# A decoder step on one core: queries turned at once, cached key products in two blocks, and the pooling state summed behind the first pooled tile

## The chip, the core and the metric

The kernel runs on one core of a Trainium2 chip. Matrix products run on TensorE (PE; its weight loads are PEld), other arithmetic on VectorE (DVE), ScalarE (ACT) and GpSimd (POOL); SyncE (SP) and the others issue transfers, which run on 16 DMA engines. The metric is the device time of one execution in microseconds (us); smaller is better.

## The reference

The reference computes one layer of a hybrid decoder for a prompt of 512 tokens and for 8 sample sequences that each add one token to 1,024 cached ones. Where the change sits, it is this (cut):

```
z = rmsnorm(x, g_mix) @ w_in          # pooling channels u, queries q, keys and values kv, gates
ext = concatenate([prefix, u])        # prefix: 15 earlier positions (state_pool) for the samples
win_sum = upto[P+1 : P+1+T] - cs[P+1-w : P+1-w+T]     # trailing sums, w = 2, 4, 8, 16
y_pool = einsum('btgc,gcd->btgd', win_sum / cnt - u, w_pool) * pool_scale
# samples, 8 heads on 2 key heads:
s_c = q . kvc      # compressed cached keys  -> p_c, o_c; the best blocks are chosen from p_c
s_s = q . cached keys of the chosen blocks   -> o_s
s_w = q . cache_win keys (512)               -> o_w
o = g0 * o_c + g1 * o_s + g2 * o_w
mem_kv = rmsnorm(mem_prompt, g_mem) @ w_xkv   # 256 memory tokens
```

Output projection, cross-attention and a gated MLP with a short convolution follow; they lie behind the change.

## The kernel before

Prompt and samples share each weight: a projection multiplies a weight tile of 128 x 128 with 512 prompt tokens and 8 sample tokens, in two halves of 260 columns. Numbers are kept as a high and a low part, so that each weight half is loaded (`load_in`, tile w_raw, on SyncE's queue), split into w_hi (a copy on ScalarE) and w_lo (a difference on VectorE), and then used by three products (L206): w_hi with x_hi, w_hi with x_lo, w_lo with x_hi. One tile is 8 blocks x 3 x 2 = 48 products.

The samples' cached keys come in eight pages Kt (`fetch_keys`), the window keys Wk and window values Wv by SyncE's queue, the cached values Vcmp and Vslc by GpSimd (`fetch_values`). `turn_queries` (L624) multiplies the sample queries by the compression weights, so that `cached_scores(r)` can multiply four pages of cached keys at once, on four strips of 32 rows of the array: L641 for the compressed scores (64 products), L646 for the scores of single tokens (8 products, 512 columns). `window_scores` (L662) does the same with Wk, `window_values` (L866) with Wv and the transposed weights PTw; `cmp_values` (L800, L807, L815) turns the compressed weights back into values.

The pooling group's four tiles run in the order gi = 3, 2, 1, 0. Each is projected, evicted into U, summed by doubling adds on GpSimd (4 for gi = 3, window 16), reduced by the running mean into pl_d on VectorE, and mapped by w_pool (L965) one tile later. For the samples, sums of the cached pooling state stp go to spre (L1007) and are needed by pl_d (L1013). The memory tokens' norm is taken from mrow (squares at L689) and spread to Rm; mt holds the memory tokens, and is split into mT_hi on ScalarE and mT_lo on VectorE.

The order of the work comes from generators that `merge` interleaves by their yields and weights, and a scheduler then orders each engine's instructions by what is written first and by the data they wait for. `last_on(engine)` holds an instruction behind the last one written so far for that engine, and `tc.issue_after(x)` behind x. Each queue takes its transfers in the order in which they are issued, and tiles come from pools with a few buffers.

Of the kernel before, what the change touches and what calls it, by code (L numbers as in the profile page):

```python
# [16 lines left out]
P = 128  # L17
# [3 lines left out]
NB = 8  # L21
HT = 260
# [85 lines left out]
def decoder_step(ctx: ExitStack, tc: tile.TileContext, A, O):  # L108
# [562 lines left out]
    def fetch_window_keys():  # L671
        for r in range(2):
            Wk.append(pair_tile("Wk").rearrange("p (b t) -> p b t", b=4))
            sp.dma_start(Wk[r], A["win_k_t"][:, 4 * r:4 * r + 4])

    def sample_front():
        yield from cached_scores(0)
        fetch_keys(7)
        fetch_window_keys()
        fetch_window_values(0)  # L680
        yield 3.0
        yield from window_scores()

    mrow = []

    def memory_norm():
        ssm = ptile(rp, [P, 8], "ss", bufs=2)
        for i in range(2):
            act.activation(mrow[0][:, i], mrow[0][:, i], AF.Square, accum_out=ssm[:, i:i + 1])  # L689
        vcopy(rsm, rstd_from(ssm[:, 0:2], 2))  # L690
        yield 3.0
        ps = bank("tb")
        with last_on(EN.PE):
            for i in range(2):
                pe.transpose(ps[:, i * P:(i + 1) * P], rsm[:, i:i + 1].to_broadcast([P, P]), ident)
        acopy(Rm, ps[:, 0:MEM])

    def sample_back():
        yield from cached_scores(1, 1.5)
        fetch_window_values(1)  # L700
        for ct in range(2):
            fetch_values(ct, "cmp")

# [83 lines left out]
    def cmp_values():  # L787

        PT = cmp_PT[0]
        wv = ptile(pb, [P, 8, 2, 64], "wvPT", name="wv")  # L790
        sp.dma_start(wv, A["w_cmp_t"][:, 1])
        acc = bank("s")
# [96 lines left out]
    def sample_attention():  # L889
# [12 lines left out]
        for ct in range(2):  # L902
            fetch_values(ct, "slc")
        yield from memory_norm()
        yield from cmp_values()
# [6 lines left out]
    def sample_end():  # L912
        a = sel_a[0]
        PTs = ptile(pb, [P, 16, 64], "wvPT", name="PTs")
        yield from selected_turn(a, PTs)
        new_values()
# [33 lines left out]
    def pooling():  # L950
        stp = ptile(pu, [P, 2, HT], "pl_d", bufs=4, name="stp").rearrange("p r t -> p (r t)")[:, 0:4 * NB * 15]
        stp = stp.rearrange("p (g b t) -> p g b t", g=4, b=NB)
        sp.dma_start(stp, A["state_pool_t"])
        spre = ptile(pu, [P, 4, NB], "spre")
        wpl = ptile(pu, [P, 4, P], "wpl")
        sp.dma_start(wpl, A["w_pool"][0].rearrange("g c d -> c g d"))
        ulast = ptile(pu, [P, 4, 24], "ulast")
# [10 lines left out]
        for hf in (1, 0):  # L968
            raw = raws[hf]
            for l in (1, 0):  # L970
# [17 lines left out]
                tt(u[:, 528:536].rearrange("p (r t) -> p r t", r=2), ps[:, :, 256:260], R1[:, :, 256:260], OP.mult)  # L988
                vcopy(ulast[:, gi], u[:, 512:536])
                win = 2 << gi  # L990
                cur = u[:, 0:528]
# [12 lines left out]
                if gi == 3:  # L1004
                    with last_on(EN.DVE):
                        for i in range(4):
                            dve.tensor_reduce(spre[:, i], stp[:, i, :, 16 - (2 << i):15], axis=AX.X, op=OP.add)  # L1007
# [227 lines left out]
    run(qt)  # L1235
    merge((kv_first(), 4.0), (gate_tile(w_g), 4.0), (turn_queries(), 3.0))
    raw_kv.append(load_in(12))
    fetch_keys(6)
    merge((kv_tiles(1, raw_kv[0]), 12.0), (sample_front(), 12.0))
    raw_p = load_in(2)  # L1240
    merge((kv_tiles(2, raw_kv[1]), 12.0), (sample_back(), 13.0))
    es_p0.close()
    pb, es_pb = open_pool("pb")
    pools = pooling()
    merge((sample_attention(), 24.0), ((next(pools) for _ in range(20)), 15.0))
# [532 lines left out]
```

## Time and profile before

| what | us |
|---|---|
| median of 3 runs (870.12 to 871.24) | 870.94 |
| the profiled execution's own time | 874.23 |
| its span, first to last instruction | 871.2 |
| TensorE busy | 839.8 |
| VectorE busy | 556.7 |
| ScalarE busy | 374.0 |
| GpSimd busy | 105.6 |

The profiled execution took 3.0 us more than the span that its trace shows, and 3.3 more than the median of the runs; rows of the trace are compared with the span.

### The profile page before, as it was taken

Reading aid. Unit: us, or ns where it says so; the run is one execution under the profiler, and the core shown is the slowest. Engines: PE = TensorE matmul, PEld = TensorE weight load, DVE = VectorE, ACT = ScalarE, POOL = GpSimd, SP = SyncE. Lnnn points to the kernel's source line nnn. Section 1 sums busy time; section 2 is a strip of 40 time slices with the busy share of each in tenths; the row PEclk is TensorE's granted clock in tenths of the full one; section 3 lists DMA queues with packets and bytes.
Section 4 is the critical chain, followed back from the end, with each engine's and each line's share of the span. In section 5 each row is a group of like instructions: output and inputs, shape, how many; then the busy total and the mean of one; then the engine's idle time right before and its main releaser. Section 6 shows DMA issues by size and latency. Waiting matters only on the chain.

```text
span 871.2 us, 17411 instructions
## 1 busy us (share of the span) xinstructions
PE 839.8 (96%) x7077; PEld 784.0 (90%) x7077; DVE 556.7 (64%) x1424; ACT 374.0 (43%) x692; POOL 105.6 (12%) x100
## 2 busy tenths in 40 slices
PE   8899978999999999999999999999999999999996
PEld 7897856887778799999799999999999999999995
DVE  4763427887667766888564587773367774357754
ACT  6442333566765544444243344441144342133462
POOL 4732132200000023000053000000000000000031
PEclk9989989999999999999999999999999999999997
DMA  9966964563312083577433633322233322333212
GB/s 341 285 212 229 412 247 165 149 221 112 118 64 59 4 262 129 167 241 252 136 97 128 223 105 97 97 98 77 77 90 97 98 97 98 97 94 86 63 62 98
DMA packets 108911, 126.02 MB, mean 145 GB/s; under 512 B 4680, under 2 KB 95176, under 8 KB 106640
## 3 DMA queue, kind: packets, MB, share of 16 engines
q1 hardware_dynamic: 103360, 102.37, 37.2%
q0 software_dynamic: 3600, 19.55, 6.0%
q10 hardware_dynamic: 1872, 3.00, 0.9%
q8 instruction: 55, 0.90, 0.4%
q14 instruction: 24, 0.20, 0.1%
HBM read 117.76 MB, written 10.69 MB: 147 GB/s over the span
## 4 chain that ended last, share of the span: by engine, by line
PE 83%; DMA 9%; DVE 4%; ACT 2%; issue 1%; DVEq 0%; POOLq 0%; SPq 0%; ACTq 0%
PE ps_pp L206 57%; DMA w_raw<-in_w_in_t_dram 4%; DMA w_u<-in_w_up_dram 3%; PE ps_o L1115 2%; PE ps_tb L1043 2%; PE ps_tb L1220 2%; PE ps_sc L1072 2%; PE ps_tf L1100 2%; PE ps_x L1408 1%; PE ps_x L1389 1%; PE ps_pp L1676 1%; PE ps_tb L1190 1%; DMA xrow<-in_x_row_dram 1%; PE ps_pp L1190 1%; DVE w_lo L120 1%; ACT w_hi L117 1%
## 5 line engine op out<-in xcount | busy, mean ns | idle before, releaser
L206 PE MATMUL ps_pp<-x_hi,w_hi 128*128 128x260 f32 x832 | 169.6, 284 | 0.4 <-ACT w_hi L117 0.4
L206 PE MATMUL ps_pp<-x_hi,w_lo 128*128 128x260 f32 x832 | 169.3, 284 | 0.5 <-DVE w_lo L120 0.5
L206 PE MATMUL ps_pp<-x_lo,w_hi 128*128 128x260 f32 x832 | 168.0, 283 | 0.0
L206 PEld LDWEIGHTS ps_pp<-x_hi,w_lo 128*128 128x128 f32 x832 | 128.8, 189 | 1.2 <-DVE w_lo L120 0.7
L206 PEld LDWEIGHTS ps_pp<-x_hi,w_hi 128*128 128x128 f32 x832 | 128.7, 189 | 0.9 <-ACT w_hi L117 0.6
L206 PEld LDWEIGHTS ps_pp<-x_lo,w_hi 128*128 128x128 f32 x832 | 128.1, 188 | 0.4 <-issue 0.4
L117 ACT ACTIVATE w_hi<-w_raw 128x1024 fp32r<-128x1024 f32 (+1 forms) x52 | 54.2, 1042 | 123.3 <-PE ps_pp L206 96.0
L120 DVE TENSOR_TENSOR hT<-hT,ps_pp 128x520 f32<-128x520 f32 (+1 forms) x44 | 28.4, 646 | 85.7 <-PE ps_pp L206 76.5
L117 ACT ACTIVATE w_hi<-w_u 128x1024 fp32r<-128x1024 f32 x44 | 46.7, 1061 | 77.1 <-PE ps_pp L206 65.4
L120 DVE TENSOR_TENSOR w_lo<-w_raw,w_hi 128x1024 fp32r<-128x1024 f32 (+1 forms) x52 | 64.5, 1240 | 8.4 <-ACT w_hi L117 8.0
L206 PE MATMUL ps_pp<-h_lo,w_hi 128*128 128x260 f32 x304 | 61.4, 283 | 0.0
L206 PE MATMUL ps_pp<-h_hi,w_hi 128*128 128x260 f32 x304 | 61.2, 283 | 0.0
L206 PE MATMUL ps_pp<-h_hi,w_lo 128*128 128x260 f32 x304 | 61.2, 283 | 0.0
L120 DVE TENSOR_TENSOR ext<-ps_pp,R 128x512 f32<-128x512 f32 x44 | 30.4, 691 | 45.4 <-PE ps_pp L206 45.2
L120 DVE TENSOR_TENSOR w_lo<-w_u,w_hi 128x1024 fp32r<-128x1024 f32 x44 | 53.9, 1225 | 7.3 <-ACT w_hi L117 7.1
L206 PE MATMUL ps_pp<-xn_hi,w_hi 128*128 128x260 f32 x208 | 45.6, 299 | 1.8 <-ACT w_hi L117 1.1
L206 PEld LDWEIGHTS ps_pp<-h_hi,w_hi 128*128 128x128 f32 x304 | 46.9, 188 | 0.2 <-ACT h_hi L117 0.2
L206 PEld LDWEIGHTS ps_pp<-h_hi,w_lo 128*128 128x128 f32 x304 | 46.9, 189 | 0.0
L206 PEld LDWEIGHTS ps_pp<-h_lo,w_hi 128*128 128x128 f32 x304 | 46.7, 188 | 0.0
L206 PE MATMUL ps_pp<-xn_lo,w_hi 128*128 128x260 f32 x208 | 43.8, 291 | 0.0
L206 PE MATMUL ps_pp<-xn_hi,w_lo 128*128 128x260 f32 x208 | 43.2, 288 | 0.0
L1618 POOL DMA_DIRECT2D out_ffn_t_dram<-last x1 | 0.6, 577 | 351.5 <-DVE last L114 351.5
(458 smaller groups left out, 1852.3 us busy)
## 6 DMA issues: line engine op xcount, KB each, us to landing
w_u<-in_w_up_dram SPq DMA_DIRECT2D x44, 512.0 KB, 4.3
xkr<-in_cache_mem_dram SPq DMA_DIRECT2D x16, 512.0 KB, 4.4
xvr<-in_cache_mem_dram SPq DMA_DIRECT2D x16, 512.0 KB, 7.3
w_raw<-in_w_down_dram SPq DMA_DIRECT2D x8, 1024.0 KB, 5.3
Kt<-in_k_t_dram SPq DMA_DIRECT2D x32, 128.0 KB, 2.4
w_raw<-in_w_in_t_dram SPq DMA_DIRECT2D x8, 512.0 KB, 5.2
w_raw<-in_w_xkv_dram SPq DMA_DIRECT2D x4, 1024.0 KB, 6.0
w_v<-in_w_xkv_dram SPq DMA_DIRECT2D x4, 1024.0 KB, 6.6
```

Of the source, the lines that this page charges most:

```text
L117: act.activation(o, i, AF.Copy, scale=scale)
L120: (eng or dve).tensor_tensor(o, a, b, op=op)
L206: pe.matmul(o, a[:, k, :], x[:, hf, :], start=(k == 0 and j == 0), stop=(k == kt - 1 and j == 2))
L1043: pe.matmul(ps[:, :HT], a[:, k, :], y[x][:, k, hf, :], start=(k + j == 0), stop=(k == 3 and j == 2))
L1072: pe.matmul(ss_[hl][:, 0:c0 + nk], Qst[:, h, qc], k[:, g, u, 0:c0 + nk], start=(u == 0), stop=(u == 1))
L1100: pe.transpose(pt[:, hh * P:(hh + 1) * P], pr[hh][:, kb * P:(kb + 1) * P], ident)
L1115: pe.matmul(po[hp * 64:(hp + 1) * 64, g * 256:(g + 1) * 256], Vtok[:, br, kb, g * 64:(g + 1) * 64], pTs[kb][:, hp * 256:(hp + 1) * 256], s ...
L1190: pe.matmul(ps[:, 0:MEM], a[:, k, :], x[:, k, :], start=(k == 0 and j == 0), stop=(k == 7 and j == 2))
L1220: pe.matmul(ps[i], x[:, k, ts_], w[:, kl, :], start=(k == 0 and j == 0), stop=(k == KT - 1 and j == 2))
L1389: pe.matmul(s[:, ql * MEM:(ql + 1) * MEM], a[:, 2 * h + dh, hf, ql * P:(ql + 1) * P], x[:, 2 * h + dh, :], start=(n == 0), stop=(n == 5))
L1408: pe.matmul(po, v[:, mb, dh * P:(dh + 1) * P], x[:, mb, :], start=(mb + j == 0), stop=(mb + j == 3))
L1676: pe.matmul(ps, a[:, dl, k, :], x[:, hf, :], start=(k + j == 0), stop=(k == kt - 1 and j == 2))
```

## The change

`turn_queries` is no longer merged with the first key and value projections: it runs by itself right behind the query tiles, and the seventh key page is asked for right behind it. `cached_scores(0)` is written as a block right behind the first key and value projection, then the last page, the window keys and the first window values are asked for; nine steps of the next projection tile follow (kv1), then `cached_scores(1)`, the other window values and two value pages, and then the rest of kv1 merged with `window_scores`. The loads of stp and w_pool move out of `pooling`, ahead of the third projection tile, and the load of wv moves ahead of `pooling`'s first weight load. The squares of `memory_norm` are held behind the last ScalarE instruction, and its spread (now `memory_spread`) moves into `sample_end`. The sums of stp are held behind the eviction of the first pooled tile (`u_done`) and no longer behind VectorE's last instruction.

```diff
--- before.py
+++ after.py
@@ -673,22 +673,16 @@
             Wk.append(pair_tile("Wk").rearrange("p (b t) -> p b t", b=4))
             sp.dma_start(Wk[r], A["win_k_t"][:, 4 * r:4 * r + 4])
 
-    def sample_front():
-        yield from cached_scores(0)
-        fetch_keys(7)
-        fetch_window_keys()
-        fetch_window_values(0)
-        yield 3.0
-        yield from window_scores()
-
     mrow = []
 
     def memory_norm():
         ssm = ptile(rp, [P, 8], "ss", bufs=2)
-        for i in range(2):
-            act.activation(mrow[0][:, i], mrow[0][:, i], AF.Square, accum_out=ssm[:, i:i + 1])
+        with last_on(EN.Activation):
+            for i in range(2):
+                act.activation(mrow[0][:, i], mrow[0][:, i], AF.Square, accum_out=ssm[:, i:i + 1])
         vcopy(rsm, rstd_from(ssm[:, 0:2], 2))
-        yield 3.0
+
+    def memory_spread():
         ps = bank("tb")
         with last_on(EN.PE):
             for i in range(2):
@@ -696,10 +690,6 @@
         acopy(Rm, ps[:, 0:MEM])
 
     def sample_back():
-        yield from cached_scores(1, 1.5)
-        fetch_window_values(1)
-        for ct in range(2):
-            fetch_values(ct, "cmp")
 
         vcopy(KC[:, :, 0], zS[:, 2, :])
         s = bank("s")
@@ -787,8 +777,7 @@
     def cmp_values():
 
         PT = cmp_PT[0]
-        wv = ptile(pb, [P, 8, 2, 64], "wvPT", name="wv")
-        sp.dma_start(wv, A["w_cmp_t"][:, 1])
+        wv = wvs[0]
         acc = bank("s")
         for g in range(2):
             pe.matmul(acc[g * 64:(g + 1) * 64, 0:32], peV, PT[:, :, 0, :, 4 * g:4 * g + 4], start=True, stop=False,
@@ -901,7 +890,7 @@
         yield from window_values()
         for ct in range(2):
             fetch_values(ct, "slc")
-        yield from memory_norm()
+        memory_norm()
         yield from cmp_values()
         for ct in range(2, 4):
             fetch_values(ct, "slc")
@@ -912,6 +901,8 @@
     def sample_end():
         a = sel_a[0]
         PTs = ptile(pb, [P, 16, 64], "wvPT", name="PTs")
+        yield 1.0
+        memory_spread()
         yield from selected_turn(a, PTs)
         new_values()
         yield 0.5
@@ -948,12 +939,7 @@
     y = {}
 
     def pooling():
-        stp = ptile(pu, [P, 2, HT], "pl_d", bufs=4, name="stp").rearrange("p r t -> p (r t)")[:, 0:4 * NB * 15]
-        stp = stp.rearrange("p (g b t) -> p g b t", g=4, b=NB)
-        sp.dma_start(stp, A["state_pool_t"])
         spre = ptile(pu, [P, 4, NB], "spre")
-        wpl = ptile(pu, [P, 4, P], "wpl")
-        sp.dma_start(wpl, A["w_pool"][0].rearrange("g c d -> c g d"))
         ulast = ptile(pu, [P, 4, 24], "ulast")
         raws = [load_in(0), raw_p]
 
@@ -987,6 +973,7 @@
                 tt(u[:, 16:528].rearrange("p (r t) -> p r t", r=2), ps[:, :, :256], R1[:, :, :256], OP.mult)
                 tt(u[:, 528:536].rearrange("p (r t) -> p r t", r=2), ps[:, :, 256:260], R1[:, :, 256:260], OP.mult)
                 vcopy(ulast[:, gi], u[:, 512:536])
+                u_done = next(i for i in reversed(nc.cur_bb.bb.instructions) if i.engine == EN.DVE)
                 win = 2 << gi
                 cur = u[:, 0:528]
                 sh = 1
@@ -1002,7 +989,7 @@
                                          u[:, 16:528].rearrange("p (r t) -> p r t", r=2), op0=OP.mult, op1=OP.subtract)
                 e = ptile(pu, [P, 16], "pl_e", bufs=2)
                 if gi == 3:
-                    with last_on(EN.DVE):
+                    with tc.issue_after(u_done):
                         for i in range(4):
                             dve.tensor_reduce(spre[:, i], stp[:, i, :, 16 - (2 << i):15], axis=AX.X, op=OP.add)
                 tt(e, cur[:, 16:32], cst[:, C_ICN + 16 * gi:C_ICN + 16 * gi + 16], OP.mult)
@@ -1233,14 +1220,33 @@
     for b in range(3, 6):
         fetch_keys(b)
     run(qt)
-    merge((kv_first(), 4.0), (gate_tile(w_g), 4.0), (turn_queries(), 3.0))
+    run(turn_queries())
+    fetch_keys(6)
+    merge((kv_first(), 4.0), (gate_tile(w_g), 4.0))
     raw_kv.append(load_in(12))
-    fetch_keys(6)
-    merge((kv_tiles(1, raw_kv[0]), 12.0), (sample_front(), 12.0))
+    run(cached_scores(0))
+    fetch_keys(7)
+    fetch_window_keys()
+    fetch_window_values(0)
+    kv1 = kv_tiles(1, raw_kv[0])
+    for _ in range(9):
+        next(kv1)
+    run(cached_scores(1))
+    fetch_window_values(1)
+    for ct in range(2):
+        fetch_values(ct, "cmp")
+    merge((kv1, 6.0), (window_scores(), 1.0))
     raw_p = load_in(2)
-    merge((kv_tiles(2, raw_kv[1]), 12.0), (sample_back(), 13.0))
+    stp = ptile(pu, [P, 2, HT], "pl_d", bufs=4, name="stp").rearrange("p r t -> p (r t)")[:, 0:4 * NB * 15]
+    stp = stp.rearrange("p (g b t) -> p g b t", g=4, b=NB)
+    sp.dma_start(stp, A["state_pool_t"])
+    wpl = ptile(pu, [P, 4, P], "wpl")
+    sp.dma_start(wpl, A["w_pool"][0].rearrange("g c d -> c g d"))
+    merge((kv_tiles(2, raw_kv[1]), 12.0), (sample_back(), 9.0))
     es_p0.close()
     pb, es_pb = open_pool("pb")
+    wvs = [ptile(pb, [P, 8, 2, 64], "wvPT", name="wv")]
+    sp.dma_start(wvs[0], A["w_cmp_t"][:, 1])
     pools = pooling()
     merge((sample_attention(), 24.0), ((next(pools) for _ in range(20)), 15.0))
     memory_split()
```

The instructions' order on an engine is shown at three places; rows give the line, the operation, the tiles and the shape, and xN stands for N in a row. A name's number is that of its buffer.

On ScalarE, around the copy PTw that the window products need, the order before was this (Swn, Ssl and Pc are scores, w_hi the high half of pooling's first weight, oW the window result):

```order
L117 ACTIVATE Vtok<-ps_tb 128x512
L758 ACTIVATE Swn,mc<-Swn,mc 128x513
L689 ACTIVATE mrow,ss<-mrow 128x1024
L758 ACTIVATE Ssl,mc<-Ssl,mc 128x1025
L117 ACTIVATE Pz<-Pc 32x63 x4
L117 ACTIVATE w_hi<-w_raw 128x1024
L117 ACTIVATE PTw<-ps_tb 128x512
L117 ACTIVATE PTc<-ps_tb 128x2x16 x2
L128 ACTIVATE mT_hi<-mt,vec 128x256 x4
```

The same place now (L748 is the old L758, L682 the old L689):

```order
L748 ACTIVATE Swn,mc<-Swn,mc 128x513
L117 ACTIVATE Pz<-Pc 32x63 x4
L117 ACTIVATE PTc<-ps_tb 128x2x16 x2
L117 ACTIVATE PTw<-ps_tb 128x512
L117 ACTIVATE oW<-ps_tb 128x256
L682 ACTIVATE mrow,ss<-mrow 128x1024 x2
L117 ACTIVATE w_hi<-w_raw 128x1024
L128 ACTIVATE mT_hi<-mt,vec 128x256 x2
L117 ACTIVATE pv_1806<-ps_tb 128x512
```

PTw, PTc and oW have moved ahead of w_hi, the squares of mrow have moved behind them, and a copy pv of the compressed values stands behind two of the mT_hi.

On TensorE, the second block of cached key products stood before as follows (the last of the projection products L206 around it are shown):

```order
L206 MATMUL ps_pp<-xn_hi,w_lo 128x260 x2
L646 MATMUL ps_tb<-Kt,Qbd 32x512 x8
L206 MATMUL ps_pp<-xn_hi,w_hi 128x260 x2
L206 MATMUL ps_pp<-xn_lo,w_hi 128x260 x2
L206 MATMUL ps_pp<-xn_hi,w_lo 128x260 x2
L206 MATMUL ps_pp<-xn_hi,w_hi 128x260 x2
L662 MATMUL ps_s<-Wk,Qbd 32x512 x4
L641 MATMUL ps_s<-Kt,QW 32x64 x47
L662 MATMUL ps_s<-Wk,Qbd 32x512 x4
L641 MATMUL ps_s<-Kt,QW 32x64 x17
```

Now the block begins and ends so, with projection products and one more L646 between the two pieces:

```order
L641 MATMUL ps_s<-Kt,QW 32x64 x3
L646 MATMUL ps_tb<-Kt,Qbd 32x512 x6
L206 MATMUL ps_pp<-xn_hi,w_hi 128x260 x2
...
L206 MATMUL ps_pp<-xn_hi,w_hi 128x260
L646 MATMUL ps_tb<-Kt,Qbd 32x512
L206 MATMUL ps_pp<-xn_hi,w_hi 128x260
...
L641 MATMUL ps_s<-Kt,QW 32x64 x61
L646 MATMUL ps_tb<-Kt,Qbd 32x512
L206 MATMUL ps_pp<-xn_lo,w_hi 128x260 x2
```

The eight L646, which were one piece, are now in pieces of 6, 1 and 1, and the 64 L641 in pieces of 3 and 61 where they were 47 and 17.

On VectorE, the first pooled tile's pl_d stood before behind the second tile's U (S is a score tile, spre the sums of the pooling state):

```order
L120 TENSOR_TENSOR U<-ps_pp,R 128x512
L120 TENSOR_TENSOR U<-ps_pp,R 128x8
L833 TENSOR_SCALAR S_2024<-Ssl,mc 32x4x64
L114 COPY ulast<-U 128x24
L833 TENSOR_SCALAR S_2024<-Ssl,mc 32x4x64
L1001 SCALAR_TENSOR_TENSOR pl_d<-pl_s,U 128x2x256
L1007 TENSOR_REDUCE spre<-stp 128x8 x4
L120 TENSOR_TENSOR pl_e<-pl_s,cst 128x16
L129 SCALAR_TENSOR_TENSOR mT_lo<-mt,vec,mT_hi 128x256
L120 TENSOR_TENSOR pl_d<-pl_e,U 128x16
```

Now the second tile's U stands behind it (L988 is the old L1001; the sums of stp, the old L1007, come 20 rows earlier):

```order
L988 SCALAR_TENSOR_TENSOR pl_d<-pl_s,U 128x2x256
L120 TENSOR_TENSOR pl_e<-pl_s,cst 128x16
L129 SCALAR_TENSOR_TENSOR mT_lo<-mt,vec,mT_hi 128x256
L120 TENSOR_TENSOR pl_d<-pl_e,U 128x16
L129 SCALAR_TENSOR_TENSOR mT_lo<-mt,vec,mT_hi 128x256 x2
L114 COPY pv_1934<-ps_tb 128x512
L129 SCALAR_TENSOR_TENSOR mT_lo<-mt,vec,mT_hi 128x256 x2
L114 COPY oC<-ps_s 128x32
L129 SCALAR_TENSOR_TENSOR mT_lo<-mt,vec,mT_hi 128x256 x2
L120 TENSOR_TENSOR U<-ps_pp,R 128x512
```

The whole of the first tile's pl_d has moved ahead of the eviction of the second tile, and the sums are no longer between its parts.

## Rows read from the trace of the kernel before

**Rows 1.** The page: the span, and busy time by engine.

```profile
span 871.2 us, 17411 instructions
...
PE 839.8 (96%) x7077; PEld 784.0 (90%) x7077; DVE 556.7 (64%) x1424; ACT 374.0 (43%) x692; POOL 105.6 (12%) x100
```

**Rows 2.** Stretches: start:end, length, busy us (instructions) of PE, PEld, DVE, ACT, POOL, clock, DMA share, GB/s.

```profile
61.10:67.20 6.10, 6.10 (x111) 5.18 (x110) 2.50 (x10) 1.21 (x4) 4.53 (x5) 0.51 0.84 277
...
81.00:112.20 31.20, 29.70 (x390) 25.39 (x388) 16.52 (x61) 10.06 (x20) 4.29 (x5) 1.00 1.01 402
112.20:116.30 4.10, 0.00 (x0) 0.00 (x0) 0.49 (x1) 1.57 (x4) 0.00 (x0) 0.83 1.02 422
116.30:121.70 5.40, 5.38 (x74) 4.72 (x75) 1.92 (x9) 1.84 (x6) 2.35 (x3) 0.50 0.36 91
...
138.60:141.90 3.30, 0.01 (x1) 0.01 (x1) 3.30 (x7) 1.01 (x2) 2.79 (x3) 1.00 0.95 303
141.90:145.70 3.80, 3.80 (x25) 2.95 (x26) 2.33 (x8) 1.08 (x2) 0.00 (x0) 0.55 0.72 289
...
164.40:871.20 706.80, 690.59 (x5558) 654.36 (x5558) 466.63 (x1179) 306.13 (x566) 48.01 (x42) 0.99 0.38 118
```

**Rows 3.** TensorE's timeline, 48 to 70 us: start, length, line, tiles, shapes, count.

```profile
54.96 3.33 PE L624 MATMUL ps_tb<-Qe,WT 64*128 64x64 f32 x28
...
62.71 2.15 PE L641 MATMUL ps_s<-Kt,QW 128*32 128x64 f32 x72
...
68.58 1.92 PE L646 MATMUL ps_tb<-Kt,Qbd 128*32 128x512 f32 x16
```

**Rows 4.** TensorE's timeline, 110 to 157 us; in brackets the idle ahead and what ended it.

```profile
110.48 0.33 PE L779 MATMUL ps_tb<-cst,Pz 128*128 128x128 f32 x1 [0.76 <-DVE Pz L114]
...
116.32 3.64 PE L866 MATMUL ps_s<-Wv,PTw 128*32 128x128 f32 x64 [4.12 <-ACT PTw L117]
...
125.01 1.05 PE L800 MATMUL ps_tb<-Vcmp,PTc 128*32 128x512 f32 x2
...
129.14 1.06 PE L800 MATMUL ps_tb<-Vcmp,PTc 128*32 128x512 f32 x6
...
141.89 1.83 PE L965 MATMUL ps_pp<-pl_d,wpl 128*128 128x260 f32 x4 [3.31 <-DVE pl_d L1013]
...
152.66 3.70 PE L845 MATMUL ps_s<-Vslc,PTs 128*32 128x128 f32 x128
```

**Rows 5.** ScalarE's timeline, 109 to 121 us.

```profile
109.25 1.03 ACT L117 ACTIVATE Pz<-Pc 32x63 f32<-32x63 f32 x4
114.72 1.06 ACT L117 ACTIVATE w_hi<-w_raw 128x1024 fp32r<-128x1024 f32 x1 [4.45 <-DMA w_raw<-in_w_in_t_dram]
115.69 0.58 ACT L117 ACTIVATE PTw<-ps_tb 128x512 f32<-128x512 f32 x1
...
118.43 1.71 ACT L128 ACTIVATE mT_hi<-mt,vec 128x256 fp32r<-128x256 f32 x4 [1.99 <-DMA mt<-in_mem_t_dram]
```

**Rows 6.** VectorE's timeline, 137 to 142 us.

```profile
137.81 0.55 DVE L1007 TENSOR_REDUCE spre<-stp 128x8 f32<-128x8 f32 x4
138.28 0.16 DVE L120 TENSOR_TENSOR pl_e<-pl_s,cst 128x16 f32<-128x16 f32 x1
...
138.76 1.64 DVE L120 TENSOR_TENSOR pl_d<-pl_e,U 128x16 f32<-128x16 f32 x1
...
141.69 0.15 DVE L1013 SCALAR_TENSOR_TENSOR pl_d<-pl_e,U 128x8 f32<-128x8 f32 x1
```

**Rows 7.** SyncE's queue, 79 to 107 us: start and length of the issues.

```profile
79.82 0.91 SPq L674 DMA_DIRECT2D Wk<-in_win_k_t_dram  x2
...
92.03 2.80 SPq L188 DMA_DIRECT2D w_raw<-in_w_in_t_dram  x2
...
106.46 0.33 SPq L976 DMA_DIRECT2D mt<-in_mem_t_dram  x1
```

**Rows 8.** GpSimd's timeline, 139 to 142 us.

```profile
139.28 2.20 POOL L120 TENSOR_TENSOR pl_s<-pl_s 128x525 f32<-128x525 f32 x2
```

## The prediction

> **What bounds it now.** The page's totals come first: TensorE is busy for 839.8 of 871.2 us [rows 1], so 31.4 us are idle, and a change that only moves instructions can win from those, from the clock that TensorE is granted, and from products that run alone where they could run four abreast. Cutting the span into stretches shows where this is [rows 2]. The last row, 706.8 us, is work that the change leaves in its order; everything is decided between 49 and 146 us. Two stretches there have no product in them: 112.20 to 116.30 (4.10 us) and 138.60 to 141.90 (3.30 us). Behind each the granted clock is about half: 5.40 us at 0.50 and 3.80 us at 0.55. A third slow stretch, 6.10 us at 0.51, has no idle ahead of it; the reader should see what ran there instead: products with 64 columns or fewer [rows 3].
>
> What ended the two idles is in TensorE's timeline [rows 4]: the window products (L866) waited 4.12 us for PTw, a copy on ScalarE, and the first-made of the four pooled maps (L965, for gi = 3) waited 3.31 us for pl_d from VectorE. Neither is slow work. PTw's copy takes 0.58 us, but it stands behind the split of a weight half (w_hi), which itself waited 4.45 us for its load [rows 5]: the queue's order let a copy wait for a transfer that it doesn't need. The pl_d wait is a queue on VectorE [rows 6]: four reductions of the cached pooling state (0.55), a 16-column product (0.16), a 16-column difference that took 1.64, and more behind it, all started only after the next tile's U had been evicted.
>
> The transfers are the third thing. From 81.0 to 112.2 us the DMA engines are full (share 1.01, 402 GB/s) [rows 2]; the window keys are requested at 79.82 us, the weight half at 92.03, and mt at 106.46 [rows 7], which is first used at 118.43 [rows 5].
>
> **PTw's copy moves ahead of the split.** The squares of memory_norm are now put last on ScalarE, and in the changed order Pz, PTc, PTw and oW stand ahead of them and of w_hi. PTw then waits for its transposes alone, which end with the cmp transposes near 111.0 [rows 4]; with 0.58 for the copy the window products can start near 112. That takes 4.12 off, and, since no idle precedes them, the clock's loss: 5.38 us busy at 0.50 [rows 2] is 5.38 x 0.5 = 2.7. (The price of half the clock is seen in like products: 64 of L866 took 3.64, 128 of L845, of the same shape, 3.70 [rows 4].) Ends: the wait vanishes (-6.8), or another transfer takes its place (first rival). I take -4.12 - 2.7.
>
> **The pooling reductions move up.** They are now tied to the end of the first pooled tile (gi = 3), and the whole of its pl_d stands ahead of the second tile's U. In TensorE's order L965's first use still comes behind the second tile's 48 products, so its input should be there. That takes 3.31 off and, behind it, 3.80 x 0.45 = 1.7 [rows 2]. What is late next is the second tile's U; it needs the last product of that tile anyway, and TensorE has the pooled map and value products to run in the meantime. Taken: -3.31 - 1.7; ends -5.0 and 0 if the queue is only shifted.
>
> What the reductions are put beside matters. The 1.64 us difference has the same 16 columns as the 0.16 us product before it; it ended, at 140.40, with the first of two adds on GpSimd that began at 139.28 and took 2.20 together [rows 6, 8]. So a VectorE instruction can be held for most of one add, 1.1. The first tile has four such adds, and the changed order puts the norm chain, a w_lo and two evictions (pv, pvs) beside them. The nearest row gives one add, 1.1 - 0.1 of its own work = 1.0, for an eviction that TensorE waits for; ends 0 (the evictions don't meet an add) and 4.0 (one each for four). Taken: +1.0. The Trainium skill ("SBUF — State Buffer", section "Who interferes with whom") says that VectorE and GpSimd share one pair of ports under an exclusive lock, that a VectorE instruction with two SBUF inputs meets a GpSimd read there, and that a reduction never does. By that rule the moved reductions are free and only w_lo and the chain pay, the evictions (one input) less surely, which would make this term 0 and the sum -9.8; the pair 1.64 and 0.16 agrees, but no row shows an eviction beside an add.
>
> **The value products behind mt.** On ScalarE the pv copy that the first value products (L815) need now stands behind two of the mT_hi splits, which wait for mt. TensorE comes to it some 7 us earlier than before, near 119, and mt lands at 118.43 less what the transfers gain: 0 to 1.5 us of wait. Taken: +0.75; ends 0 and 4.4 plus 2 of clock (first rival).
>
> **Groups of four strips.** L646 and L800 run four products abreast on strips of the array: a group cost 1.05 for two records of it and 1.06 for six [rows 4], so a group cut by other work pays anew; eight of L646 took 0.96 (16 in 1.92) [rows 3]. The changed order cuts the second tile's eight L646 into 6, 1 and 1, where they were two groups of four: four groups for two, 2 x 0.96 = +1.9. It saves one of seven L800 groups: -1.05. Both are read from the order, and where the pieces meet in the array they may overlap more; ends 0 and these.
>
> **Queries and key products.** The turns (L624) run 16 in a row, then 29 projection products, then 64 key products (L641) in a row, where both had been strewn among projection products. The number of products is the same. What can differ is the clock: 6.10 us at 0.51 [rows 2] cost 6.10 x 0.49 = 3.0. I take it as unchanged, with ends 0 (the 29 products hold the clock up) and twice as much. Behind the key products, the last key page is requested as TensorE passes them, and Wk behind it, about 3 us sooner than 79.82. cached_scores(1) ends 7 us sooner, so the last window values and two value pages are asked for sooner too, and the full train of transfers (402 GB/s) can start, but not run, faster. The wait of the cmp transposes, 0.76 [rows 4], grows to about 1.2 as TensorE's filler is used up earlier: +0.45 (estimate from that row; ends -0.76 and +2).
>
> The pooling state and w_pool loads move ahead of mrow, and wv ahead of the weight half. Issuing them costs SyncE nothing that anyone waits for: two weight issues stand 2.80 us in its row [rows 7] far ahead of their use. Cover gone, each MB ahead of the weight half costs 1 / 0.402 = 2.5 us of its landing; that is in the first rival.
>
> **Sum.** -4.12 - 2.7 - 3.31 - 1.7 - 1.05 + 1.0 + 0.75 + 1.9 + 0.45 = -8.8. On the profiled execution's own time, 874.23 (its span is 871.2, so 3.0 lie around it), that is 865.4. The median of the runs is 870.94, 3.3 lower; taken off there: **862.1**. A measurement of this kernel can tell about 0.2%, 1.7 us, from no change.
>
> **Rivals.** (1) *The transfers become the bound.* The reordering takes waits away where TensorE was ahead of the train, so it meets the train elsewhere: at raw_p's second half (first pooled tile) or at mt. For it: the DMA share is 1.01 over 31.2 us, and two Vslc pages are requested earlier, into the same train. Against: mt is asked for ahead of them. Price: an idle of about 3 us with half a clock behind it for 4, so 3 + 2 = 5 back, net about -4: 865 to 869. [...] Chance 0.20.
>
> (2) *Better than the sum.* Neither the cut groups nor the ports cost, and the clock stays up between 49 and 68: -1.9 - 1.0 - 3.0 more, 850 to 856. For it: the turns are no longer next to L593's narrow products. Chance 0.12.
>
> (3) *Slower: the clock.* Sixteen turns and 64 key products in one piece are the work beside which the clock fell to 0.51 [rows 2, 3]. If it stays down behind them, each microsecond of it costs half of one. To undo -8.8 and add 1.7 it needs (8.8 + 1.7) x 2 = 21 us more at half clock than before; the longest stretch now is 6.1, and wide products bring it back by 67.2. Time 873 or more. Chance 0.08.
>
> (4) *It does nothing*: waits move by as much as they shrink, 869.2 to 872.7. Against it: PTw's wait is an accident of the queue, and the order shows it gone. Chance 0.05.
>
> **Chances.** The forecast (856 to 865) 0.55, its own range. Cases below 853.5 and above 869 hold 0.2 together, so the range is 853.5 to 869.0. Faster 0.87 (forecast, 1 and 2), same 0.05 (4), slower 0.08 (3).
>
> **What would show it.** Right: L866 starts within 1 us of its transposes and the clock after it is 1.0; no wait of 3 us for pl_d; L646 in four groups; the 706.8 us tail as it was. Wrong: an idle over 2 us before a product that waits for w_hi, w_lo or for a pv copy behind mT_hi (then rival 1), or a half clock of 10 us and more from 55 on (rival 3). The steps least sure are the two transfer meetings, raw_p and mt, which no row of before can show.

## The result, and the profile after

The changed kernel takes 861.12 us (median of 4 runs, 858.84 to 861.94) where the kernel before took 871.09 (4 runs): a ratio of 0.9883, 95% interval 0.9867 to 0.9898, or 10.0 us less. The forecast was 862.1, 8.8 less. Two more measurements of the changed kernel (e4 and e12 below) give 0.9877 and 0.9890.

The profiled execution took 858.84 us, the fastest of its four, and stands 15.4 below the profiled one of before, so the pair of traces shows more than the medians do. 1.4 us of it lie ahead of everything that the change touches: TensorE's first compression product (L593) starts at 49.34 before and at 47.92 now. From there to the start of the last ps_pp product of mT_hi and w_hi for the memory keys (L1190, now L1177) it is 177.9 - 49.3 = 128.6 us before and 164.9 - 47.9 = 117.0 now, 11.6 less; in the traces of e4 and e12, of the same kernel, it is 119.8 and 119.6, or 8.8 and 9.0 less. Those two are the fairer picture, and where this trace differs from them it is said. Behind that product the span is as it was: 693.3 us before, 692.2 here, 692.6 and 692.7 in e4 and e12.

The page of the changed kernel, against [rows 1]:

```profile
span 857.1 us, 17417 instructions
...
PE 833.6 (97%) x7077; PEld 777.6 (91%) x7077; DVE 558.6 (65%) x1424; ACT 373.8 (44%) x692; POOL 106.2 (12%) x100
```

Stretches of it, with the columns of [rows 2]:

```profile
52.80:57.20 4.40, 4.40 (x26) 4.04 (x26) 2.05 (x9) 2.46 (x11) 1.98 (x3) 0.61 0.41 126
104.00:110.00 6.00, 5.70 (x95) 5.15 (x94) 2.44 (x16) 1.88 (x9) 0.94 (x1) 1.00 1.01 400
110.00:116.90 6.90, 6.90 (x49) 3.87 (x47) 3.33 (x10) 3.52 (x6) 4.35 (x6) 1.00 1.02 422
116.90:119.20 2.30, 0.31 (x3) 0.11 (x5) 2.30 (x9) 1.50 (x4) 1.93 (x2) 1.00 0.70 292
119.20:132.00 12.80, 12.71 (x131) 8.93 (x131) 10.21 (x33) 7.14 (x15) 2.06 (x3) 1.00 0.31 101
```

The 4.10 us without a product are gone, and the clock is 1.00 from 104 to 132 us. What is left is one short idle, 116.90 to 119.20, in which TensorE works 0.31 of 2.30 us. The half clock between the query turns and the key products is there as before (0.61 over 4.40 us here; 0.54 over 7.00 in e12, where [rows 2] have 0.51 over 6.10). The key products behind it, now in one piece, run at full clock: from 60 to 68 us it is 1.00.

TensorE's timeline shows the ends of it, against [rows 3, 4] (L855 is the old L866, L804 the old L815, L951 the old L965):

```profile
72.18 1.89 PE L646 MATMUL ps_tb<-Kt,Qbd 128*32 128x512 f32 x12
...
75.76 1.05 PE L646 MATMUL ps_tb<-Kt,Qbd 128*32 128x512 f32 x2
...
82.46 1.02 PE L646 MATMUL ps_tb<-Kt,Qbd 128*32 128x512 f32 x2
...
106.17 0.63 PE L848 MATMUL ps_tb<-cst,Swn 128*128 128x128 f32 x4 [0.30 <-DVE Swn L886]
...
107.57 1.95 PE L855 MATMUL ps_s<-Wv,PTw 128*32 128x128 f32 x64
...
119.14 0.66 PE L804 MATMUL ps_s<-pv,wv 128*64 128x32 f32 x16 [1.99 <-ACT pv L117]
...
130.82 1.04 PE L951 MATMUL ps_pp<-pl_d,wpl 128*128 128x260 f32 x4
```

The 64 window products start at 107.57 without a wait and take 1.95 us where they took 3.64. The pooled map at 130.82 waits for nothing and takes 1.04 where it took 1.83. The second block's L646 take 1.89 + 1.05 + 1.02 = 3.96 us where they took 1.93 (TensorE's timeline of the kernel before):

```profile
82.90 1.93 PE L646 MATMUL ps_tb<-Kt,Qbd 128*32 128x512 f32 x16
```

One wait is new: 1.99 us ahead of the first value products, for a copy pv on ScalarE, and ScalarE's rows say why, against [rows 5]:

```profile
106.83 0.60 ACT L117 ACTIVATE PTw<-ps_tb 128x512 f32<-128x512 f32 x1 [0.23 <-PE ps_tb L848]
...
113.09 1.04 ACT L117 ACTIVATE w_hi<-w_raw 128x1024 fp32r<-128x1024 f32 x1
...
117.70 0.91 ACT L128 ACTIVATE mT_hi<-mt,vec 128x256 fp32r<-128x256 f32 x2 [3.57 <-DMA mt<-in_mem_t_dram]
118.51 0.57 ACT L117 ACTIVATE pv<-ps_tb 128x512 f32<-128x512 f32 x1
```

PTw is copied at 106.83, w_hi follows at 113.09 and waits for no load, and the pv copy stands behind two mT_hi that begin when mt has landed, at 117.70. mt was used first at 118.43 before, 0.7 us later, while TensorE now ends the second block's key products (L641) at 82.62 where it ended them at 89.87. On SyncE's queue, against [rows 7], Wk is asked for 3.3 us sooner, the weight half 5.6 later and mt at the same time:

```profile
76.54 0.91 SPq L674 DMA_DIRECT2D Wk<-in_win_k_t_dram  x2
...
97.64 1.66 SPq L188 DMA_DIRECT2D w_raw<-in_w_in_t_dram  x2
106.52 0.33 SPq L962 DMA_DIRECT2D mt<-in_mem_t_dram  x1
```

Here the traces of e4 and e12 differ. Wk is asked for at 79.13 and 80.18 there, which is no clear gain on 79.82; the weight half at 100.12 and 101.22; mt at 108.69 and 109.64, and it is first used at 120.08 and 120.72, 1.7 and 2.3 us later than before. So the earlier front does not bring mt in sooner. ScalarE's row in e12:

```profile
120.72 0.91 ACT L128 ACTIVATE mT_hi<-mt,vec 128x256 fp32r<-128x256 f32 x2 [3.07 <-DMA mt<-in_mem_t_dram]
```

VectorE's rows beside the first pooled tile's adds, against [rows 6] (L223 is a step of the memory norm on two columns):

```profile
115.09 1.44 DVE L223 TENSOR_SCALAR rs_i<-rs_ms 128x2 int32<-128x2 int32 x1
...
116.57 0.98 DVE L224 TENSOR_SCALAR rs_y<-rs_i 128x2 int32<-128x2 int32 x1
...
117.82 1.11 DVE L120 TENSOR_TENSOR rs_t<-rs_t,rs_hx 128x2 f32<-128x2 f32 x1
...
119.10 1.21 DVE L120 TENSOR_TENSOR w_lo<-w_raw,w_hi 128x1024 fp32r<-128x1024 f32 x1
...
125.83 0.69 DVE L988 SCALAR_TENSOR_TENSOR pl_d<-pl_s,U 128x512 f32<-128x512 f32 x1
```

The adds themselves, on GpSimd, against [rows 8]:

```profile
113.49 1.07 POOL L120 TENSOR_TENSOR pl_s<-U 128x527 f32<-128x527 f32 x1 [2.35 <-DVE U L120]
...
116.47 2.44 POOL L120 TENSOR_TENSOR pl_s<-pl_s 128x521 f32<-128x521 f32 x2
```

L223 takes 1.44 us beside them and a product of two columns 1.11; where no add runs L223 takes 0.17 (in e1, below).

In e12 the new wait is 1.49 us (TensorE's timeline):

```profile
122.16 0.66 PE L804 MATMUL ps_s<-pv,wv 128*64 128x32 f32 x16 [1.49 <-ACT pv L117]
```

and it has half a clock behind it, 0.60 over 4.10 us, which the first trace has not (stretches of e12; e4 has 0.58 over 4.10):

```profile
55.00:62.00 7.00, 7.00 (x35) 6.37 (x36) 2.55 (x11) 2.53 (x11) 3.80 (x5) 0.54 0.56 162
122.10:126.20 4.10, 4.04 (x27) 2.52 (x27) 3.44 (x16) 4.03 (x11) 0.32 (x1) 0.60 0.07 28
```

### The profile page after: what moved, and what is told of

Its sections match the earlier page's. It is cut to its first block, busy times and chain, and to the rows that moved or that the text cites. A ratio compares the mean times of both kernels' runs of the same rounds, so it can differ in the third digit from the quotient of the medians.

```text
span 857.1 us, 17417 instructions
## 1 busy us (share of the span) xinstructions
PE 833.6 (97%) x7077; PEld 777.6 (91%) x7077; DVE 558.6 (65%) x1424; ACT 373.8 (44%) x692; POOL 106.2 (12%) x100
## 4 chain that ended last, share of the span: by engine, by line
PE 85%; DMA 6%; DVE 4%; ACT 3%; issue 1%; DVEq 0%; POOLq 0%; ACTq 0%; SPq 0%
PE ps_pp L206 60%; DMA w_u<-in_w_up_dram 3%; PE ps_o L1102 2%; PE ps_tb L1030 2%; PE ps_tb L1207 2%; PE ps_sc L1059 2%; PE ps_tf L1087 2%; PE ps_x L1414 1%; PE ps_x L1395 1%; DMA mt<-in_mem_t_dram 1%; DMA out_kv_t_dram<-zk 1%; PE ps_pp L1682 1%; PE ps_tb L1177 1%; DVE w_lo L120 1%; ACT w_hi L117 1%; PE ps_s L1452 1%
## 5 line engine op out<-in xcount | busy, mean ns | idle before, releaser
L206 PE MATMUL ps_pp<-x_hi,w_lo 128*128 128x260 f32 x832 | 169.2, 284 | 0.5 <-DVE w_lo L120 0.5
L206 PE MATMUL ps_pp<-x_hi,w_hi 128*128 128x260 f32 x832 | 169.4, 284 | 0.0
L206 PE MATMUL ps_pp<-x_lo,w_hi 128*128 128x260 f32 x832 | 167.9, 283 | 0.0
L206 PEld LDWEIGHTS ps_pp<-x_hi,w_lo 128*128 128x128 f32 x832 | 128.7, 188 | 1.1 <-DVE w_lo L120 0.7
L206 PEld LDWEIGHTS ps_pp<-x_hi,w_hi 128*128 128x128 f32 x832 | 128.7, 188 | 0.3
L206 PEld LDWEIGHTS ps_pp<-x_lo,w_hi 128*128 128x128 f32 x832 | 128.1, 188 | 0.4 <-issue 0.4
L117 ACT ACTIVATE w_hi<-w_raw 128x1024 fp32r<-128x1024 f32 (+1 forms) x52 | 54.2, 1042 | 119.6 <-PE ps_pp L206 99.5
L206 PE MATMUL ps_pp<-h_lo,w_hi 128*128 128x260 f32 x304 | 61.3, 283 | 0.0
L206 PE MATMUL ps_pp<-h_hi,w_hi 128*128 128x260 f32 x304 | 61.1, 282 | 0.0
L206 PE MATMUL ps_pp<-h_hi,w_lo 128*128 128x260 f32 x304 | 61.1, 282 | 0.0
L206 PEld LDWEIGHTS ps_pp<-h_hi,w_hi 128*128 128x128 f32 x304 | 46.9, 188 | 0.2 <-ACT h_hi L117 0.2
L206 PEld LDWEIGHTS ps_pp<-h_hi,w_lo 128*128 128x128 f32 x304 | 46.9, 189 | 0.0
L206 PEld LDWEIGHTS ps_pp<-h_lo,w_hi 128*128 128x128 f32 x304 | 46.8, 188 | 0.0
L206 PE MATMUL ps_pp<-xn_hi,w_hi 128*128 128x260 f32 x208 | 45.0, 294 | 1.3 <-ACT w_hi L117 1.1
L206 PE MATMUL ps_pp<-xn_lo,w_hi 128*128 128x260 f32 x208 | 43.1, 286 | 0.5 <-DVE xn_lo L129 0.5
L1067 ACT ACTIVATE prob<-prob,mx 128x384 f32<-128x384 f32 (+3 forms) x64 | 35.4, 556 | 17.2 <-DVE mx L1065 16.8
```

What stands on the lines that cost most here:

```text
L117: act.activation(o, i, AF.Copy, scale=scale)
L206: pe.matmul(o, a[:, k, :], x[:, hf, :], start=(k == 0 and j == 0), stop=(k == kt - 1 and j == 2))
L1067: act.activation(p[:, 0:nk], p[:, 0:nk], AF.Exp, bias=mx[:, hh:hh + 1], scale=-1.0, accum_out=sm[:, hh:hh + 1])
```

## The experiments

Twelve runs on three chips. On the one of e4 to e7 the kernel before took 871.4 us and on the one of e11 and e12 871.1; on the one of e1 to e3 and e8 to e10 it took 896.2 to 896.4 (the last section tells where it loses them). The kernel before has no trace from this slower chip. Ratios are to the kernel before on the same chip, with a 95% interval, and each trace is of one execution.

**e1: the window products' copies on VectorE** (kernel before)

```diff
-        acopy(PTw.rearrange("p a b -> p (a b)"), pt)
+        vcopy(PTw.rearrange("p a b -> p (a b)"), pt)
...
-                (acopy if i else vcopy)(PT[:, 2 * r:2 * r + 2, i],
+                vcopy(PT[:, 2 * r:2 * r + 2, i],
```

> The kernel before, with the copies PTw and PTc on VectorE, so that no product before the first pv copy waits for ScalarE's w_hi. My theory (the window products' wait is a queue behind an unneeded split): L866 starts near 112.3 instead of 116.3, its 64 products take about 1.9 us instead of 3.64, and 4.1 + 2.7 = 6.8 us go, less a wait of about 1 us at the first pv copy, which stands behind mT_hi: 871.1 - 5.8 = about 865.3. Rival (the transfers are the bound): TensorE meets mt instead, the first L815 waits 3 us or more with half the clock behind it, and the time is 868 to 870.

Ratio 1.0028 (1.0010 to 1.0045): slower by 2.5 us. TensorE's timeline:

```profile
135.78 1.95 PE L866 MATMUL ps_s<-Wv,PTw 128*32 128x128 f32 x64
143.38 0.69 PE L873 MATMUL ps_tb<-cst,oS 128*128 128x128 f32 x2 [4.59 <-DVE oS L114]
```

VectorE's:

```profile
131.40 0.17 DVE L223 TENSOR_SCALAR rs_i<-rs_ms 128x2 int32<-128x2 int32 x1
...
138.95 1.23 DVE L120 TENSOR_TENSOR w_lo<-w_raw,w_hi 128x1024 fp32r<-128x1024 f32 x1 [3.29 <-ACT w_hi L117]
...
142.91 0.42 DVE L114 COPY oS<-ps_s 128x256 f32<-128x256 f32 x1
```

L866 runs without a wait in 1.95 us, as my theory had it, and then the next step waits 4.59: oS, which VectorE evicts, stands behind w_lo, which waits 3.29 for w_hi and so for the same weight half. Neither theory named this place. The wait was not PTw's alone: two engines' queues held a copy behind that split, and freeing one moves the wait behind 2 us of products. (Why it is slower, and not only as fast, the trace doesn't settle; on the same chip, e2 has 4.09 us of wait at L866, 0.5 less.)

**e2: the sums alone** (kernel before), and **e3: both**

```diff
                 vcopy(ulast[:, gi], u[:, 512:536])
+                u_done = next(i for i in reversed(nc.cur_bb.bb.instructions) if i.engine == EN.DVE)
...
-                    with last_on(EN.DVE):
+                    with tc.issue_after(u_done):
```

> The kernel before, with only the sums of the pooling state held behind U. The first tile's pl_d still stands behind the second tile's U on VectorE. My theory (pl_d's place behind U makes the wait, not the sums): the sums (0.55) and their followers leave the queue, L965 waits 2 us or more still, and the time falls by 0 to 2: 869 to 871. Rival (the sums are the wait): L965 waits under 0.5 us, the clock behind stays up, and 3.3 + 1.7 = 5 go: 866.

> Both edits on the kernel before. If the two waits are independent, the gains of the two runs add within 1 us (my theory: about 865.3 less 0 to 2). Rival: TensorE arrives 6 us sooner at L965 while VectorE's queue waits for the same U and POOL adds, so the second wait grows and the sum is 2 us or more short of the two.

e2: 0.9962 (0.9946 to 0.9979), 3.4 us less. e3: 0.9981 (0.9956 to 1.0006); e1 and e2 together give 0.9990, inside an interval that is 4.5 us wide, so they may add, but within 1 us is not shown. The wait at oS is there in e3 as well (5.16). TensorE's timeline in e2:

```profile
162.94 1.14 PE L965 MATMUL ps_pp<-pl_d,wpl 128*128 128x260 f32 x4 [0.53 <-DVE pl_d L120]
...
165.66 0.66 PE L815 MATMUL ps_s<-pv,wv 128*64 128x32 f32 x16 [1.21 <-DVE pv L114]
```

L965 waits 0.53 where it waited 3.31, with no half clock behind it, and L815 1.21 behind it. My theory falls: pl_d still stands behind U, and the sums with their followers (the 16-column difference beside an add, the sums' own chain) were most of the wait.

**e4: the changed kernel again**, the base of the next three

> The changed kernel as it is, on the chip of the next three. Expected near 861.1, as before. It is the base for them.

861.42 us, 0.9877 (0.9851 to 0.9904).

**e5: the second block's L646 whole** (changed kernel; the first block's, whole already, are held too)

```diff
-        for hf in range(2):
-            for c in range(4):
-                pe.matmul(pss[hf][32 * c:32 * c + 32], Qbd[...], Kt[...], ...)
+        with last_on(EN.PE):
+            for hf in range(2):
+                for c in range(4):
+                    pe.matmul(pss[hf][32 * c:32 * c + 32], Qbd[...], Kt[...], ...)
```

> The changed kernel, with the second block's eight L646 held behind its 64 L641, so that they run as two groups of four instead of four groups. My theory (a cut group costs a whole one): TensorE saves two groups of 1.0 us, 2.0 us less than the changed kernel. Rival (the pieces of 6, 1 and 1 fill time in which TensorE would wait for the last key page): the 61 L641 and the scores behind them come later, a wait of 1 us or more appears at Pz or Swn, and the time is the same within 0.5 us or worse.

0.9951 (0.9932 to 0.9970): 5.3 us slower than e4. TensorE's timeline:

```profile
86.92 1.07 PE L663 MATMUL ps_s<-Wk,Qbd 128*32 128x512 f32 x8 [0.37 <-DMA Wk<-in_win_k_t_dram]
...
103.16 0.80 PE L206 MATMUL ps_pp<-xn_hi,w_hi 128*128 128x260 f32 x2 [2.77 <-ACT w_hi L117]
```

ScalarE's:

```profile
102.06 1.06 ACT L117 ACTIVATE w_hi<-w_raw 128x1024 fp32r<-128x1024 f32 x1 [12.06 <-DMA w_raw<-in_w_in_t_dram]
```

The groups do run whole, and TensorE then waits 0.37 for Wk and 2.77 for the first w_hi of pooling, which itself waited 12.06 for its load. In e4 that w_hi starts at 101.89, and TensorE still has projection products then. Counted from L593 the load is 1.5 us later here (54.5 against 52.9), which is part of the wait. Behind it the clock is 0.57 over 4.00 us, and the second value products wait 2.10 where the first waited 1.54 in e4. The rival holds, at another place than it named: the 2.03 us of the cut groups are saved and not won. The size of the loss is not explained: this trace is of the fastest of the twelve executions (864.40), its stretch from L593 to the memory keys is 2.5 us longer than in e4, and the medians lie 5.3 apart.

**e6: the pv copy ahead of mT_hi** (changed kernel)

```diff
+            if q == 0:
+                pv_done.append(next(i for i in reversed(nc.cur_bb.bb.instructions) if i.engine == EN.Activation))
...
-        for k in range(KT):
-            split(mT[0][:, k], mT[1][:, k], mt[0][:, k], scale=vec[:, 24 + k:25 + k])
+        with tc.issue_after(pv_done[0]):
+            for k in range(KT):
+                act.activation(mT[0][:, k], mt[0][:, k], AF.Copy, scale=vec[:, 24 + k:25 + k])
+        for k in range(KT):
+            dve.scalar_tensor_tensor(mT[1][:, k], mt[0][:, k], vec[:, 24 + k:25 + k], ...)
```

> The changed kernel, with the mT_hi splits held behind the first pv copy on ScalarE. My theory: L804's wait of 1.99 us, which ends when mt has landed and two mT_hi are done, goes, and the time falls by 1.5 to 2.0. Rival: TensorE then meets mt's landing or the second pvs copy one step later (it stands behind two mT_hi), so that less than 0.7 us is won.

862.33 us, 0.9895 (0.9871 to 0.9918), against 861.42 for e4: nothing won. TensorE's timeline:

```profile
122.14 0.66 PE L807 MATMUL ps_s<-pv,wv 128*64 128x32 f32 x16
...
127.44 0.66 PE L807 MATMUL ps_s<-pv,wv 128*64 128x32 f32 x16 [1.30 <-DVE pv L114]
```

VectorE's:

```profile
120.49 1.44 DVE L223 TENSOR_SCALAR rs_i<-rs_ms 128x2 int32<-128x2 int32 x1
...
124.51 1.22 DVE L120 TENSOR_TENSOR w_lo<-w_raw,w_hi 128x1024 fp32r<-128x1024 f32 x1
...
126.69 0.69 DVE L114 COPY pv<-ps_tb 128x512 f32<-128x512 f32 x1
```

The first L807 (122.14) no longer waits; the second waits 1.30 for a pv copy on VectorE, which comes behind the memory norm's chain, slowed by the adds, and a w_lo. So the next late thing was the queue that the prediction priced at +1.0.

**e7: both** (changed kernel)

> Both edits on the changed kernel. My theory: 2.0 + 1.8 = 3.8 us less than the changed kernel, near 857.3. Rival: with both, TensorE comes to the pv copies 2 us sooner and waits there for the transfers, and the gain is no more than that of the better of the two.

866.78 us, 0.9932 (0.9907 to 0.9957): worse than the changed kernel, like e5. Neither edit is an improvement. Its trace, again of the fastest of twelve (861.14), has the waits of e5 (0.41 for Wk, 2.71 for w_hi) and no longer a stretch than e4 (119.0 us), so it doesn't show what the others lose.

**e8: the turns merged as before** (changed kernel)

```diff
-    run(turn_queries())
-    fetch_keys(6)
-    merge((kv_first(), 4.0), (gate_tile(w_g), 4.0))
+    merge((kv_first(), 4.0), (gate_tile(w_g), 4.0), (turn_queries(), 3.0))
     raw_kv.append(load_in(12))
+    fetch_keys(6)
```

> The changed kernel, with the query turns strewn among the first projections and the seventh key page asked for behind them, as before the change. My theory: the stretch at half clock comes back to its old place and length (6 to 7 us where the changed kernel has about 4), which costs 1.4 us; the last key page is asked for about 3 us later, and mt lands no later than 1 us: 1 to 3 us more than the changed kernel. Rival (turning at once does nothing): within 0.7 us of it.

0.9910 (0.9885 to 0.9934), on the slower chip, where the changed kernel was not run; e9 and e10 there have 0.9865 and 0.9869, and the changed kernel had 0.9877 to 0.9890 on the others. The intervals overlap: a loss of 2 to 4 us is likely and not shown.

**e9: the squares not held** (changed kernel)

```diff
-        with last_on(EN.Activation):
-            for i in range(2):
-                act.activation(mrow[0][:, i], mrow[0][:, i], AF.Square, accum_out=ssm[:, i:i + 1])
+        for i in range(2):
+            act.activation(mrow[0][:, i], mrow[0][:, i], AF.Square, accum_out=ssm[:, i:i + 1])
```

> The changed kernel, without the hold of the memory squares on ScalarE. The prediction's step says that the hold is what puts PTw ahead of w_hi: then L855 would wait for w_hi and the time would rise by 4 us or more. The order says otherwise: PTw still stands ahead of w_hi, but six mT_hi stand ahead of the first pv copy. My theory now: L855 starts within 0.5 us of its place, L804 waits 3 to 4 us instead of 1.99 and may bring half a clock: 1 to 4 us more.

0.9865 (0.9821 to 0.9908). ScalarE's timeline:

```profile
127.96 1.06 ACT L681 ACTIVATE mrow<-mrow 128x1024 f32<-128x1024 f32 x1 [4.75 <-DMA mrow<-in_mem_row_dram]
...
129.02 1.03 ACT L117 ACTIVATE Pz<-Pc 32x63 f32<-32x63 f32 x4
```

TensorE's:

```profile
130.10 0.47 PE L768 MATMUL ps_tb<-cst,Pz 128*128 128x128 f32 x1 [4.39 <-ACT Pz L117]
```

The first square waits 4.75 us for mrow, Pz stands behind it, and TensorE waits 4.39 at Pz's transpose, with half a clock behind it (0.59 over 7.50 us; the window products take 3.29). So the hold does take a wait away, but another than the prediction said: PTw stays ahead of w_hi without it. The wait that I expected at the value products didn't come. The time can't tell what the hold is worth: the interval is 8 us wide, and up to the memory keys TensorE waits nowhere behind this in the trace (in e10 it waits 0.53 + 0.79 + 1.44 + 0.47 there).

**e10: the sums late again** (changed kernel; the second hunk of e2's diff, undone)

> The changed kernel, with the sums of the pooling state back behind VectorE's last instruction. pl_d of the first tile still stands ahead of the second tile's U. My theory (the place of pl_d against U decides, not the sums): no wait at L951 above 0.5 us, the time within 0.7 us of the changed kernel. Rival (the sums decide): L951 waits 1 us or more, and 1 to 5 us come back.

0.9869 (0.9843 to 0.9894). L951 has no wait; four of 0.47 to 1.44 us stand ahead of it, at L862 and L804, and so bring TensorE 3.2 us later to it. As for e8, the time can't be set against the changed kernel's. My theory on the wait holds here, and with e2 it reads: either edit alone takes most or all of the wait at the pooled map away.

**e11: the orders alone** (kernel before), with **e12: the changed kernel** beside it. The edits are those of e2 and of e6, and this one:

```diff
         acopy(oW.rearrange("p r t -> p (r t)"), pt[:, 0:256])
+        held.extend(next(i for i in reversed(nc.cur_bb.bb.instructions) if i.engine == e) for e in (EN.Activation, EN.DVE))
...
+                if gi == 1:
+                    with ExitStack() as es_w:
+                        for ins in held:
+                            es_w.enter_context(tc.issue_after(ins))
+                        w = split_w(raw[:, l])
+                else:
+                    w = split_w(raw[:, l])
```

> The kernel before, its queries, key products and loads as they were, with three holds alone: the third pooled weight's split behind oW and oS on ScalarE and VectorE, mT_hi behind the first pv copy, and the sums of the pooling state behind U. My theory (the change wins by what stands ahead of what on ScalarE and VectorE behind 110 us, not by the turns and the key products): L866, L873 and L965 wait under 1 us each, no half clock behind them, and the ratio to the kernel before is 0.987 to 0.991, that of the changed kernel within 0.3%. Rival (the earlier front and the moved loads are needed): the train of transfers is met elsewhere, a wait of 2 us or more with half a clock behind it comes back, and the ratio is 0.994 or more.

> The changed kernel beside it on the same chip: 0.988 of the kernel before, on this chip too.

e11: 861.94 us, 0.9888 (0.9858 to 0.9919); e12: 862.57 us, 0.9890 (0.9857 to 0.9923). The same, within intervals of 3 us to either side. TensorE's timeline in e11 (L870, L877, L970 are the old L866, L873, L965):

```profile
112.35 1.96 PE L870 MATMUL ps_s<-Wv,PTw 128*32 128x128 f32 x64
...
115.17 0.38 PE L877 MATMUL ps_tb<-cst,oS 128*128 128x128 f32 x2
...
132.44 1.14 PE L970 MATMUL ps_pp<-pl_d,wpl 128*128 128x260 f32 x4 [0.53 <-DVE pl_d L120]
```

The queries, key products and loads are as before, and the whole gain is there, from what stands ahead of what behind 110 us. Of its three holds only that of the sums was run alone (e2); what the split's hold or mT_hi's gives by itself is not shown.

## Why the prediction was right

*PTw's copy moves ahead of the split (-4.12 - 2.7).* Size right: L855 starts without a wait and at full clock. The cause as put was wrong twice. The hold of the squares doesn't move PTw (e9), and PTw is only half of it: VectorE's w_lo stood ahead of oS, and e1, which frees PTw alone, waits there. The changed order has both halves of the third weight's split behind oW and oS, and e11 shows that this, with the sums and mT_hi, is enough. Which part of the change moves the split is not shown. (That w_hi, in the order shown ahead of the prediction, is the high half of the third pooled tile's weight; the text there calls it the first's.)

*The pooling reductions (-3.31 - 1.7).* Size right, and the place too; but the step had both moves as one cause, and either is nearly enough: the sums alone win 3.4 us (e2), pl_d's place alone leaves no wait at the map (e10).

*The ports (+1.0).* The rows are as foreseen, 1.44, 0.98 and 1.11 us for instructions of two columns beside the adds, yet no eviction was slowed and in the changed kernel TensorE waits for none of it. The Trainium skill ("SBUF — State Buffer", section "Who interferes with whom") has the sums free of this; the four of them take 0.24 + 0.20 + 0.26, which agrees. The Trainium skill, in the same section, also has an instruction with one input in SBUF free of it unless it runs in a mode with two ports; L223 has one input and took 1.44, and no run here shows in which mode.

*The value products behind mt (+0.75).* Mis-sized: 1.99, 1.54 and 1.49 in the three traces, and in the last two half a clock behind it (4.10 us at 0.60 in e12, 1.6 us). The step let mt land at 118.43 or sooner, with TensorE there near 119. In e4 and e12 TensorE is there at 119.98 and 120.67, but mt is first used at 120.08 and 120.72: later than before, not sooner. This and the ports' term are not a sum: both run under the same wait, and e6 shows the second (1.30) as soon as the first is gone.

*Groups of four strips (+1.9, -1.05).* Right in the trace: +2.03, and six L789 groups for seven. e5 shows that +2.03 was filler: without it TensorE waits for raw_p's load instead, and nothing is won.

*Queries and key products (0, +0.45).* The half clock is unchanged in e4 and e12 (0.54 over 7.00 against 0.51 over 6.10) and shorter in the first trace. The transposes wait 0.31 in e12 where they waited 0.76: -0.45 for +0.45. The prediction read the slow 6.10 us as products with 64 columns or fewer; ten L206 of 260 columns run among them, and the clock is back at 67.2 us while L641 of 64 columns run, so the rows don't show that wide products bring it back, as rival (3) says.

*The sum*, for e12: -4.12 - 2.7 - 3.31 - 1.7 - 1.05 + 2.03 - 0.45 + 1.49 + 1.6 = -8.2, and two waits of before that have gone, 0.73 ahead of a projection product at 91.39 and 0.46 at pvs: -9.4; the stretch is 9.0 shorter. The two large terms are right; that -8.8 came so close is luck, because the errors at mt, the ports and the small waits cancel.

*The rivals.* (1) was partly right: TensorE does meet the train at mt, but for 1.5 to 2 us with 1.6 of clock in e12, not 3 + 2; e5 shows it at raw_p. (2) and (3) did not come: the cut groups cost their 2 us, and the clock is low between the turns and the key products for about as long as before.

## What to carry to other kernels

A wait that ends at a copy belongs to the queue ahead of it: before moving the copy, look at every engine on which an instruction of the same late transfer stands ahead of work that the critical engine needs, and move all of them or none (e1 against e11). Costs that run under one wait are not added; price the longest, and name the next. Work on the bound engine that looks wasteful may be filler in front of a transfer, so undo it alone before counting it as a gain (in e5 two such microseconds were saved and none won).

## What the runs showed of the hardware

The kernel before took 896 us on one chip and 871 on the two others. The traces from the slow one, none of them of the kernel before, show where: between 38 and 56 us, and in the key products near 72 to 88, TensorE has gaps that end in "issue", that is, in nothing that the profile shows, and the clock is low around them. TensorE's waits between 36 and 94 us in e10 (total, times, longest):

```profile
PE ps_pp L206 <- issue: 3.8, 10, 0.8
PE ps_s L641 <- issue: 3.0, 4, 1.2
```

Two stretches of e10:

```profile
38.00:56.00 18.00, 13.89 (x62) 11.92 (x61) 5.85 (x14) 2.68 (x4) 8.62 (x9) 0.63 0.51 141
66.00:96.00 30.00, 26.52 (x286) 21.30 (x285) 10.05 (x32) 8.24 (x24) 7.56 (x8) 0.83 0.44 135
```

The same two of e12, the changed kernel on another chip:

```profile
38.00:56.00 18.00, 18.00 (x149) 17.80 (x148) 11.66 (x26) 6.59 (x11) 8.50 (x8) 0.96 0.75 237
66.00:96.00 30.00, 29.95 (x369) 22.22 (x362) 9.54 (x28) 5.84 (x12) 3.37 (x4) 1.00 0.74 279
```

TensorE runs 62 matmuls in the first stretch where it runs 149, and the cause isn't known. With the turns merged (e8) the second stretch has a clock of 0.66 and 243 matmuls; with the turns at once (e10) 0.83 and 286. So on that chip the change's first part may have a worth that it hasn't on the chip where e11 does without it; no run shows it.
